# Ordering each engine's instructions with the timeline model instead of the default machine model: a delta-rule block, two MLP stages and an RWKV block on one core

## The chip, the cores and the metric

The kernel runs on 1 core of one Trainium2 chip. Its time is the device time of one execution in microseconds (us). The core has five engines that each work off a fixed list of instructions in order: TensorE (PE in the profile; its weight loads are shown as PEld), VectorE (DVE), ScalarE (ACT), GpSimd (POOL) and SyncE (SP), which here only issues transfers. Engines wait for one another through semaphores.

## What is computed

A sequence of 256 tokens of width 1024, in float32, goes through two models one after the other. All weights are float32 and are read once.

```
# first_block (DEPTH 1)
u = rms_norm(h, norm_mix);  proj = u @ w_in
pool_out = pool_mixer(proj[:, :512])                  # trailing means, a small matmul per group
q, k, v  = silu(causal_conv(proj[:, 512:2048]))       # 4 heads of 128
gdn_out  = gated_delta_net(q, k, v, z, a, b)          # chunked, a triangular solve per chunk
h = h + concat(pool_out, gdn_out) @ w_out
h = h + square(relu(rms_norm(h) @ w_up)) @ w_down     # 1024 -> 4096 -> 1024
x = rms_norm(h)
# second_block (DEPTH 2)
x = x + spatial_gating(rms_norm(x));  x = x + mlp(rms_norm(x))
x = x + rwkv7(rms_norm(x));           x = x + mlp(rms_norm(x))
out = rms_norm(x)
...
# rwkv7, per head and token t
sa = S @ (-kk_t);  S = S * w_t + sa kka_t^T + v_t k_t^T;  y_t = S @ r_t
```

## The kernel before

**Matmuls.** Each float32 operand of a large matmul is split into a high part in TensorE's float32r type and a low part that holds the rest; `split` (L205) makes them, the high part with a cast on ScalarE (L222), the low part with a subtraction on VectorE (L227; for eight RWKV weights on ScalarE and a transfer of GpSimd, L224 and L225). `mm3` (L230) then adds three matmuls: high x high (L231) and the two products of a high and a low part (L232, L233). Weights come in tiles of 1 MB from `load_ws` (L184) and `load_as` (L190), whose transfers are issued on SyncE. Raw weights, split weights, activations and PSUM tiles come from pools with a fixed number of buffers, so a load or a split waits until an older tile of its pool is released.

**Stages.** `block1` (L475) runs the projections and the delta rule on the first 150 us. The delta rule is a chain of small dependent steps on TensorE, VectorE and ScalarE: decay matrices, a triangular inverse by blocks (`eliminate`, L918; the steps Y, Z and ZT, L796 to L814), chunk state, output. The rest of the projections, the pool mixer and part of the output projection are a generator, `dense`; `fill()` pulls a few matmuls of it after each step of the chain. `mlp` (L410) runs 16 chunks of 256 hidden columns; `up(c)` is written before `down(c - 1)`. `sgu` (L968) is the spatial gating stage. `rwkv` (L1147) does the projections and decays, then a recurrence in four windows: `before`, `state`, `solve`, `update` and `output` (L1672 to L1719), each for two halves of the heads, with ScalarE copies from PSUM between the steps (L1688, L1698, L1719); its fillers are the generators `dense` and `late`. `fin` (L1721) normalises the output per head, `half_xt` (L249) transposes it, `out_mm` (L1807) projects it.

**What sets the order.** The code is written in one sequence. The framework's `TileContext` (L1919) records each instruction with its dependences and, when the context closes, decides the list of each engine: it plays the program through a model of the machine and lets each engine take, among the instructions that are ready for it in the model, the one written first. Buffers of a pool are handed out in the same pass, and semaphore waits are put in afterwards. The engines then run these lists as they are; nothing is reordered on the chip.

## Time and profile before

| | us |
|---|---|
| median of 3 runs | 1080.01 |
| lowest and highest | 1079.74 and 1084.63 |
| the profiled execution | 1082.05 |
| its span, first to last instruction | 1080.30 |
| mean granted TensorE clock, share of full speed | 0.982 |

The profile is of one execution. Its rows name an engine, a line of the kernel, the operation, and the output tile with its inputs; in a table by stretch each engine has its busy time and, in brackets, its instructions, and PEclk is the granted TensorE clock as a share of 2.4 GHz. Matmuls are pipelined, so their rows overlap: the time between two starts is what one costs.

### The profile page before, as it was taken

The page shows a single profiled execution, that of the slowest core. Times are in us where ns is not written, and L with a number is a line of the kernel's source. Part 1 is how long each engine was busy: PE and PEld are TensorE (multiplying, and loading weights), DVE is VectorE, ACT ScalarE, POOL GpSimd, SP SyncE. Part 2 cuts the span into 40 slices and gives each one's busy share as a digit, 9 for nine tenths or more (in the row PEclk, how much of TensorE's full clock was granted, in tenths as well). Part 3 has the DMA queues.
Part 4 walks back from the last instruction along what each step waited for, and adds up shares of the span by engine and source line. Part 5 has one row for each costly group of instructions (what it writes and reads, how often), then busy time and mean ns, then how long its engine had stood idle before and what let it go on. Part 6 is the DMA issues. An engine that isn't in the chain of part 4 may idle for free.

```text
span 1080.3 us, 19680 instructions
## 1 busy us (share of the span) xinstructions
PE 1049.7 (97%) x8138; PEld 939.3 (87%) x8138; DVE 726.5 (67%) x1267; ACT 560.6 (52%) x834; POOL 61.8 (6%) x102
## 2 busy tenths in 40 slices
PE   8999999999999999999999999999999989999996
PEld 6899878988898999889999998999768869999985
DVE  5889665556557886666685556998943875555565
ACT  5745454454446554455464446864535635444452
POOL 3100000000002000000000001024200000000000
PEclk9999999999999999999999999998998999999998
DMA  7343186555564745555576561445623244655531
GB/s 246 121 157 118 42 309 213 184 189 171 181 195 121 246 154 174 188 166 180 172 241 191 193 196 33 112 139 139 156 60 118 80 156 159 192 195 188 188 132 40
DMA packets 123318, 173.63 MB, mean 161 GB/s; under 512 B 6638, under 2 KB 100827, under 8 KB 122972
## 3 DMA queue, kind: packets, MB, share of 16 engines
q1 hardware_dynamic: 121930, 168.11, 48.7%
q0 software_dynamic: 1152, 4.19, 2.0%
q8 instruction: 64, 1.05, 0.4%
q14 instruction: 26, 0.21, 0.1%
q10 hardware_dynamic: 146, 0.07, 0.0%
HBM read 167.12 MB, written 1.05 MB: 156 GB/s over the span
## 4 chain that ended last, share of the span: by engine, by line
PE 83%; DVE 11%; ACT 3%; issue 1%; DMA 1%; POOL 1%; SPq 0%; ACTq 0%; POOLq 0%; DVEq 0%
PE m1a L231 3%; PE m3h L232 3%; PE m3h L233 3%; PE m1a L233 3%; PE m1a L232 3%; PE m3h L231 3%; PE m1h L232 3%; PE m2h L232 3%; PE m2h L233 3%; PE m1h L233 3%; PE m1h L231 3%; PE m2h L231 3%; PE m2a L231 3%; PE m2a L232 3%; PE m2a L233 3%; PE m3a L232 3%
## 5 line engine op out<-in xcount | busy, mean ns | idle before, releaser
L231 PE MATMUL m1h<-m1xh,m1uh 128*128 128x256 f32 x256 | 73.3, 287 | 0.0
L233 PE MATMUL m3h<-m3xh,m3ul 128*128 128x256 f32 x256 | 72.2, 282 | 0.5 <-DVE m3ul L227 0.5
L232 PE MATMUL m3h<-m3xl,m3uh 128*128 128x256 f32 x256 | 72.1, 282 | 0.3 <-DVE m3xl L391 0.3
L231 PE MATMUL m3h<-m3xh,m3uh 128*128 128x256 f32 x256 | 72.1, 282 | 0.0
L232 PE MATMUL m1h<-m1xl,m1uh 128*128 128x256 f32 x256 | 71.8, 281 | 0.2 <-DVE m1xl L391 0.2
L233 PE MATMUL m2h<-m2xh,m2ul 128*128 128x256 f32 x256 | 71.7, 280 | 0.0
L232 PE MATMUL m2h<-m2xl,m2uh 128*128 128x256 f32 x256 | 71.6, 280 | 0.0
L233 PE MATMUL m1h<-m1xh,m1ul 128*128 128x256 f32 x256 | 71.6, 280 | 0.0
L231 PE MATMUL m2h<-m2xh,m2uh 128*128 128x256 f32 x256 | 71.5, 280 | 0.0
L227 DVE TENSOR_TENSOR m3ul<-m3u,m3uh 128x1024 fp32r<-128x1024 f32 x32 | 39.2, 1225 | 47.3 <-ACT m3uh L222 47.3
L227 DVE TENSOR_TENSOR m1ul<-m1u,m1uh 128x1024 fp32r<-128x1024 f32 x32 | 39.2, 1225 | 44.9 <-ACT m1uh L222 44.8
L227 DVE TENSOR_TENSOR m2ul<-m2u,m2uh 128x1024 fp32r<-128x1024 f32 x32 | 39.1, 1225 | 35.8 <-ACT m2uh L222 35.8
L222 ACT CAST m1uh<-m1u 128x1024 fp32r<-128x1024 f32 x32 | 33.7, 1053 | 52.1 <-PE m1h L232 50.4
L222 ACT CAST m3uh<-m3u 128x1024 fp32r<-128x1024 f32 x32 | 33.5, 1048 | 51.8 <-PE m3h L232 50.0
L222 ACT CAST m2uh<-m2u 128x1024 fp32r<-128x1024 f32 x32 | 33.5, 1050 | 47.9 <-PE m2h L232 45.4
L227 DVE TENSOR_TENSOR m2dl<-m2d,m2dh 128x1024 fp32r<-128x1024 f32 x32 | 39.2, 1225 | 26.1 <-ACT m2dh L222 26.1
L227 DVE TENSOR_TENSOR m3dl<-m3d,m3dh 128x1024 fp32r<-128x1024 f32 x31 | 38.0, 1225 | 24.9 <-ACT m3dh L222 24.9
L227 DVE TENSOR_TENSOR m1dl<-m1d,m1dh 128x1024 fp32r<-128x1024 f32 x31 | 37.9, 1224 | 22.0 <-ACT m1dh L222 22.0
L222 ACT CAST m2dh<-m2d 128x1024 fp32r<-128x1024 f32 x32 | 33.6, 1050 | 33.4 <-PE m2a L233 29.9
L222 ACT CAST m1dh<-m1d 128x1024 fp32r<-128x1024 f32 x31 | 32.4, 1047 | 35.3 <-PE m1a L233 24.4
L231 PE MATMUL m2a<-m2dh,m2fh 128*128 128x512 f32 x128 | 50.1, 391 | 0.0
L222 ACT CAST m3dh<-m3d 128x1024 fp32r<-128x1024 f32 x31 | 32.7, 1054 | 33.4 <-PE m3a L233 31.6
(708 smaller groups left out, 3542.5 us busy)
## 6 DMA issues: line engine op xcount, KB each, us to landing
m1u<-in_w_up_dram SPq DMA_DIRECT2D x16, 1024.0 KB
m1d<-in_w_down_dram SPq DMA_DIRECT2D x16, 1024.0 KB, 4.9
m2u<-in_ffn_w_dram SPq DMA_DIRECT2D x16, 1024.0 KB, 6.5
m2d<-in_ffn_w_dram SPq DMA_DIRECT2D x16, 1024.0 KB, 5.5
m3u<-in_ffn_w_dram SPq DMA_DIRECT2D x16, 1024.0 KB
m3d<-in_ffn_w_dram SPq DMA_DIRECT2D x16, 1024.0 KB, 4.9
win<-in_w_in_dram SPq DMA_DIRECT2D x10, 1024.0 KB
sv<-in_sgu_w_in_dram SPq DMA_DIRECT2D x8, 1024.0 KB, 5.7
```

Source lines behind the costliest of these rows:

```text
L222: act.copy(hv, src)
L227: lo.tensor_tensor(out=lv, in0=src, in1=hv.bitcast(F32), op=ALU.subtract)
L231: pe.matmul(out, lhsT=lh, rhs=rh, start=first, stop=False)
L232: pe.matmul(out, lhsT=lh, rhs=rl, start=False, stop=False)
L233: pe.matmul(out, lhsT=ll, rhs=rh, start=False, stop=last)
```

## The change

One argument of the context is set. The code of the kernel, its tiles and its pools are the same; the model on which the framework plays the program when it decides each engine's list, and hands out the buffers, is another one, the framework's timeline model instead of its default machine model.

```diff
-    with tile.TileContext(nc) as tc:
+    with tile.TileContext(nc, schedule_with_timeline_sim=True) as tc:
         tile_two_blocks(tc, args)
```

## Rows read from the trace of the kernel before

**Rows 1.** The page: span and instructions, and each engine's busy time
```profile
span 1080.3 us, 19680 instructions
PE 1049.7 (97%) x8138; PEld 939.3 (87%) x8138; DVE 726.5 (67%) x1267; ACT 560.6 (52%) x834; POOL 61.8 (6%) x102
```

**Rows 2.** Busy time by stretch: us; PE, PEld, DVE, ACT, POOL (instructions); PEclk, DMA, GB/s
```profile
12.00:160.00 148.00, 142.30 (x1044) 130.63 (x1043) 119.80 (x307) 80.33 (x157) 10.89 (x19) 0.98 0.47 151
160.00:330.00 170.00, 170.00 (x1070) 150.99 (x1069) 96.83 (x107) 80.57 (x93) 0.95 (x1) 1.00 0.59 191
402.00:660.00 258.00, 257.75 (x1668) 233.81 (x1667) 163.67 (x193) 129.66 (x168) 2.85 (x11) 1.00 0.57 181
660.00:900.00 240.00, 227.94 (x2701) 196.17 (x2700) 180.88 (x397) 137.57 (x246) 34.88 (x50) 0.94 0.40 113
900.00:1066.00 166.00, 166.00 (x1063) 151.44 (x1063) 91.99 (x91) 78.31 (x90) 0.00 (x0) 1.00 0.52 170
1066.00:1080.30 14.30, 5.08 (x21) 3.50 (x20) 8.28 (x25) 3.77 (x10) 0.00 (x0) 0.80 0.20 74
```

**Rows 3.** The same view for the six low-clock stretches: one, and their sum
```profile
818.60:828.90 10.30, 10.23 (x133) 9.74 (x125) 4.05 (x6) 7.74 (x15) 0.00 (x0) 0.50 0.04 12
...
sum 34.20, PE 33.82 PEld 29.57 DVE 21.50 ACT 15.09 POOL 6.99; mean PE 5.64 PEld 4.93 DVE 3.58 ACT 2.52 POOL 1.16
```

**Rows 4.** First MLP: TensorE in time (start, length), groups of splits, one load
```profile
200.25 0.28 PE L231 MATMUL m1h<-m1xh,m1uh 128*128 128x256 f32 x1
200.36 0.28 PE L232 MATMUL m1h<-m1xl,m1uh 128*128 128x256 f32 x1
...
206.13 0.39 PE L232 MATMUL m1a<-m1dl,m1fh 128*128 128x512 f32 x1
206.37 0.40 PE L233 MATMUL m1a<-m1dh,m1fl 128*128 128x512 f32 x1
...
L222 ACT CAST m1uh<-m1u 128x1024 fp32r<-128x1024 f32 x32 | 33.7, 1053 | 52.1 <-PE m1h L232 50.4 <-DMA m1u<-in_w_up_dram 1.2 <-PE mo L233 0.2
L227 DVE TENSOR_TENSOR m1ul<-m1u,m1uh 128x1024 fp32r<-128x1024 f32 x32 | 39.2, 1225 | 44.9 <-ACT m1uh L222 44.8
...
m1d<-in_w_down_dram SPq DMA_DIRECT2D x16, 1024.0 KB, 4.9
```

**Rows 5.** VectorE and TensorE in time at the end of RWKV
```profile
866.14 1.22 DVE L227 TENSOR_TENSOR m3ul<-m3u,m3uh 128x1024 fp32r<-128x1024 f32 x1
...
870.78 0.68 DVE L349 TENSOR_TENSOR res<-ra,res 128x512 f32<-128x512 f32 x1
871.38 0.68 DVE L1740 TENSOR_TENSOR tBK<-tBK,V 128x512 f32<-128x512 f32 x1
...
872.21 0.63 PE L252 MATMUL yt<-ident,tBK 128*128 128x128 f32 x4 [1.99 <-DVE tBK L1740]
```

**Rows 6.** Waits of TensorE: us in total, times, longest
```profile
PE pj L233 <- DVE wil L227: 1.6, 4, 0.8
...
PE kk L1347 <- ACT sq L1343: 1.1, 1, 1.1
```

**Rows 7.** Groups of block one's triangular inverse: busy us, mean ns, idle before
```profile
L801 ACT COPY Y<-Y 128x512 f32<-128x512 f32 x6 | 3.4, 589 | 5.9 <-PE Y L799 5.9
L814 DVE TENSOR_TENSOR U<-ZT,U 128x512 f32<-128x512 f32 x6 | 4.0, 686 | 0.0
L809 DVE TENSOR_TENSOR X<-Z,X 128x512 f32<-128x512 f32 x4 | 2.7, 686 | 1.6 <-PE Z L807 1.5
```

**Rows 8.** Groups of the RWKV recurrence on ScalarE
```profile
L1719 ACT COPY tBK<-PD 64x512 f32<-64x512 f32 x8 | 4.6, 581 | 5.1 <-PE PD L1717 5.1
L1698 ACT COPY tBK<-Ud 64x512 f32<-64x512 f32 x8 | 4.6, 580 | 4.1 <-PE Ud L1696 4.0
```

**Rows 9.** ScalarE in time at block one's logarithms
```profile
33.43 1.28 ACT L699 ACT_TABLE_LOAD   x1
34.73 0.21 ACT L699 ACTIVATE gl<-ge 128x8 f32<-128x8 f32 x1
```

## The prediction, made before the change was run

> **What bounds the kernel now.** I read the page first: TensorE is busy for 1049.7 of 1080.3 us, VectorE for 67% and ScalarE for 52% [rows 1]. Then the busy time of each engine by stretch [rows 2]. Three stretches hold the three MLPs and most of the spatial gating stage (160 to 330, 402 to 660 and 900 to 1066 us): TensorE idles 0.25 us in 594. Two stretches are different. From 12 to 160 us (block one: projections and the gated delta rule) it idles 148.0 - 142.3 = 5.7 us; from 660 to 900 us (the RWKV mixer) 240.0 - 227.9 = 12.1 us. The rest of the 30.6 us of idle time is the tail after 1066 us (14.3 - 5.1 = 9.2), one chain from the last matmul to the store, and 3.4 us at the start and between the stages.
>
> The granted clock is the other loss. It is at 1.2 instead of 2.4 GHz in six stretches, 34.2 us in all, every one of them inside or just behind the two loose stretches [rows 3]; were all of it matmul time, it would cost half, 17.1 us. So the two loose stretches, 388 of 1080 us, hold 17.8 us of idle time and up to 17.1 us of slow clock: some 35 us for which the order of instructions can be held responsible.
>
> **The change, part by part.** No instruction, tile or buffer is added or taken away. The framework plays the program through a model of the machine and gives each engine, whenever that engine is free in the model, the earliest-written instruction that is ready there; that sequence is then each engine's fixed queue. With another model other instructions are ready first. What can move is seen by laying the instruction lists of the compiled kernel before beside the order in which the code writes them. TensorE's list leaves the written order 96 times among block one's 807 instructions, 87 times among RWKV's 1707, 38 times among spatial gating's 992, and 34 times in all three MLPs (3545). VectorE's does so 199 times in block one and 248 in RWKV. All five queues are re-made: SyncE's loads and GpSimd's few operations too.
>
> *The MLP stretches: 0 us.* One chunk is 48 matmuls of 256 columns, issued 0.12 us apart, and 24 of 512, 0.23 us apart [rows 4]: 5.7 + 5.6 = 11.3 us of back-to-back TensorE work, while a chunk's four casts and four subtractions take 4 x 1.05 on ScalarE and 4 x 1.22 us on VectorE. What hides their order is that they are early: ScalarE waits for TensorE to release a weight buffer (50.4 us in all for the first MLP's up weights), not the other way [rows 4]. A weight tile that is released when its matmuls end is needed again one chunk less those matmuls later, 11.3 - 2.8 = 8.5 us; cast and subtraction take 2.3, so 6 us of disorder on ScalarE or VectorE cost nothing. If that cover were gone, each microsecond beyond it would come 46 times.
>
> *SyncE's queue.* A load sits there until its buffer is free, and everything behind it waits too; who waits for that is ScalarE's cast. A load lands 4.9 us after its issue and ScalarE waited 1.2 us in all for the first MLP's up weights [rows 4]. Two neighbouring loads swapped cost nothing; I take 0 and keep the bad case as a rival.
>
> *Block one and RWKV: the terms that count.* Here the written order alternates dependent steps with filler matmuls that have nothing to do with them. What a wrong place costs is on show at 866 us. The two normalisations of the RWKV output run on VectorE, which is never idle there; a 1.22 us subtraction for the next MLP's weights and a 0.68 us residual add stand in the middle of them, and TensorE, out of other work, waits 1.99 us for the first one's last step [rows 5]. Put later, they would have saved most of the 1.99. Other long waits are for a VectorE or ScalarE step too, 1.1 and 1.6 us [rows 6]. From above: no order gets back more than the 17.8 us of idle time plus the clock's 17.1. Typically a model that is nearer to the chip would get back the waits in which something movable stood ahead; I put that at a third of the idle time, 6 us.
>
> From below there is no such bound. The dependent chains are long and each hand-over is bare when its filler has been used up elsewhere. Block one's triangular inverse has 6 copies of 0.59 us on ScalarE and 10 adds of 0.69 us on VectorE [rows 7]; these 16 are now mostly under the other half's matmuls and the filler, since TensorE idles for only 5.7 us of the stage. RWKV's recurrence has three ScalarE copies for each window and half, 24 of 0.58 us (two of the three rows of 8 are in [rows 8]), with the output projection, the gates and the other half as cover. Bare, a chain costs 16 x 0.65 = 10.4 us in block one and 24 x 0.58 = 13.9 us in RWKV. I take a third of each, 3.5 + 4.6 = 8.1 us, since each chain has three sources of cover (other half, filler, next window) and a re-made order is likely to lose about one of them in places; the ends are 0 and 24.3. The low-clock stretches lie in and behind these same chains, so I add one more of 10.3 us at half rate, 5.1 us, as the row at 818 us has it (the one at 750 us is as long) [rows 3]; ends 0 and 10.3.
>
> *ScalarE's function tables.* In block one two logarithms sit between exponentials and hyperbolic tangents, and each change of table is a load of 1.28 us [rows 9]. A tangent of the filler placed between the two logarithms adds two loads, 2.6 us on ScalarE, which is busy for 80.3 of that stage's 148 us [rows 2]; bounds 0 and 2.6, I take 0. The Trainium skill ("ScalarE: Activation LUTs", What ACT_TABLE_LOAD costs and the rule to batch calls by set) speaks against mixing them and gives about 2.66 us for every switch, the load and a drain. By that the sum would be 2 x 2.66 = 5.3 us instead of 2.6, as an estimate. The trace shows the load's 1.28 us and the next activation starting right behind it, so the lower figure agrees better.
>
> *The sum.* Bare hand-overs 8.1, slow clock 5.1, recovered waits -6, all else 0: +7.2 us. The profiled execution took 1082.05 us, 1.75 us outside its span, and lies 2.0 us above the median of the runs shown (1080.01); the sum belongs on 1082.05, which makes 1089.3, and 1087.2 beside the median. I forecast 1087.
>
> **A measure that doubts the bound.** TensorE's busy share is 95% in RWKV, but its weight loads are busy for only 196 of 240 us, 82%, against 151 of 170 us, 89%, in an MLP where it never stops [rows 2]. By that yardstick RWKV has 240 x (1 - 0.82/0.89) = 19 us to give instead of 12. The Trainium skill ("Perfetto Trace Analysis", Identifying the Most-Contended Engine) calls matmul busy time a poor measure of headroom and prefers the share of weight loading; by it the rival that comes next has more room. The trace bears that out only partly, since RWKV's many small tiles load fewer weights by nature.
>
> **The rivals.** *The nearer model wins.* The new order keeps the normalisations together, moves the reductions behind more filler and puts the clock's two 10 us stretches under denser work. It gets back half of the idle time, 8.9 us, and one of those stretches, 5.1 us: 1080.0 - 14 = 1066; with only the idle half, 1071. For it: the waits of [rows 5, 6] are mistakes of placement, which a faithful model would not make. Against it: VectorE is busy for 181 of 240 us in RWKV and without a gap around 866 us, so part of the waiting is work, not order. I put it at 1070.
>
> *Nothing that counts.* TensorE is near its limit, both models agree on what is ready, or the flag changes lists only where there is cover: 1080, within 5 us. For it: 594 us in which TensorE waits for nothing. This takes in the case that the order comes out the same.
>
> *Loads in the wrong order.* This one is slower by far: in the model a transfer is quick, so a load that must wait for a buffer is put ahead of one that TensorE needs next. Place: SyncE's queue in the MLPs; it decides once the load comes over 6 us late. Price: one microsecond beyond the cover in each of 46 chunks, 46 us, 1126. Against it: ScalarE's waits for loads are near 0 today.
>
> **How the numbers follow.** The forecast, bare hand-overs outweighing recovered waits: 0.40. Wrong loads: 0.05. Nothing that counts: 0.27. The nearer model wins: 0.28. The measurement of this kernel can tell about 0.5%, 5.4 us, from no change. So slower by over 0.5% is 0.45, within it 0.27, faster 0.28. As both signs have much of the chance, the forecast's own range is without the clock term 8.1 - 6 = 2 above the median, 1082, and with both chains bare and nothing else 1080.0 + 24.3 = 1104. The range for 8 times in 10 reaches down to 1068, below which I leave half of the nearer model's case away (about 0.1), and up to 1106, above which lie the wrong loads and a forecast with both chains bare and a slower clock (about 0.1).
>
> **What would show it.** If the forecast is right, the MLP stretches stay at full TensorE time with the same spacing, TensorE's idle time grows in block one or RWKV in waits for ScalarE copies and VectorE adds of the chains, and the low-clock time grows past 34 us. If the nearer model wins, idle time falls below 12 us together in those two stretches and the 1.99 us wait is gone. If loads are the matter, ScalarE waits for transfers in the MLPs. The prediction is wrong in its base if the MLP stretches change length, since all of them are costed at nothing.

## The result: 5% slower, and what the profile after shows

| | before | after |
|---|---|---|
| median, us | 1079.88 | 1134.64 |
| lowest and highest, us | 1078.69 to 1084.63 | 1133.28 to 1137.53 |
| ratio, 95% interval | | 1.0499, 1.0473 to 1.0524 |
| span of the profiled execution, us | 1080.3 | 1133.8 |
| mean granted TensorE clock | 0.982 | 0.963 |

The change costs 54.8 us. The forecast was 1087 us with a range up to 1106: the sign was right, the size was not.

The page of the changed kernel, the lines that answer to [rows 1]. The same instructions run, and all engines but TensorE are busy for as long as before (within 3 us).

```profile
span 1133.8 us, 19693 instructions
PE 1075.8 (95%) x8138; PEld 960.9 (85%) x8138; DVE 729.1 (64%) x1267; ACT 560.6 (49%) x834; POOL 64.2 (6%) x102
```

Busy time by stage, first the kernel before and then the changed one. The borders are the first matmul of the next stage (for the first and the third MLP that of the up projection, `m1h` and `m3h`): block one up to 148.0 (after: 169.3) us, then the first MLP, the gating stage, the second MLP and RWKV. Columns as in [rows 2].

```profile
0.00:148.00 148.00, 139.71 (x966) 122.94 (x967) 114.27 (x294) 77.56 (x147) 16.01 (x36) 0.98 0.48 153
148.00:331.80 183.80, 183.56 (x1173) 163.88 (x1172) 106.64 (x130) 89.84 (x112) 0.95 (x1) 1.00 0.61 197
331.80:477.80 146.00, 145.47 (x1040) 135.41 (x1039) 109.91 (x197) 78.55 (x110) 7.27 (x6) 1.00 0.55 175
477.80:659.40 181.60, 181.35 (x1177) 165.40 (x1176) 114.06 (x135) 94.66 (x121) 2.50 (x8) 1.00 0.57 181
659.40:890.00 230.60, 219.36 (x2634) 188.06 (x2633) 175.43 (x383) 132.09 (x236) 35.07 (x51) 0.94 0.41 116
```

```profile
0.00:169.30 169.30, 147.86 (x967) 130.01 (x968) 116.70 (x295) 77.36 (x147) 14.72 (x36) 0.93 0.43 140
169.30:355.60 186.30, 185.24 (x1177) 164.99 (x1176) 107.66 (x131) 89.73 (x112) 0.95 (x1) 1.00 0.60 190
355.60:508.90 153.30, 148.50 (x1037) 137.72 (x1035) 109.12 (x196) 78.72 (x110) 6.85 (x6) 0.98 0.54 171
508.90:695.70 186.80, 183.57 (x1177) 166.72 (x1176) 114.69 (x135) 93.98 (x121) 2.49 (x8) 0.99 0.54 171
695.70:943.00 247.30, 230.46 (x2636) 197.76 (x2635) 175.54 (x383) 133.04 (x236) 39.17 (x51) 0.91 0.39 108
```

The slow clock, the answer to [rows 3]: there were six stretches at 1.2 GHz, 34.2 us; now there are fifteen, 78.5 us (without the tail, where the clock is low in both kernels). The longest, and the sum:

```profile
862.60:876.20 13.60, 9.09 (x140) 8.64 (x142) 3.20 (x4) 6.96 (x13) 0.00 (x0) 0.50 0.40 143
...
sum 78.50, PE 71.23 PEld 62.84 DVE 50.40 ACT 24.27 POOL 5.29; mean PE 4.75 PEld 4.19 DVE 3.36 ACT 1.62 POOL 0.35
```

From these rows: idle time is length less TensorE's busy time; slow clock is what of the stretches lies in the stage, and half of what it grew by is its cost if all of it is matmul time.

| stage | longer by, us | TensorE idle | more idle | slow clock | half of its growth |
|---|---|---|---|---|---|
| block one | 21.3 | 8.3 to 21.4 | 13.1 | 6.8 to 23.9 | 8.6 |
| first MLP | 2.5 | 0.2 to 1.1 | 0.8 | 0 | 0 |
| gating | 7.3 | 0.5 to 4.8 | 4.3 | 0 to 6.8 | 3.4 |
| second MLP | 5.2 | 0.3 to 3.2 | 3.0 | 0 to 3.5 | 1.8 |
| RWKV | 16.7 | 11.2 to 16.8 | 5.6 | 27.3 to 44.3 | 8.5 |
| third MLP, tail | 0.5 | 10.1 to 10.6 | 0.6 | 0 | 0 |
| sum | 53.5 | 30.6 to 58.0 | 27.4 | 34.2 to 78.5 | 22.2 |

27.4 + 22.2 = 49.6 of the 53.5 us. This counts twice what TensorE idles within the slow stretches; TensorE's busy time in them grew by 71.2 - 33.8 = 37.4 us, half of it is 18.7, and the sum 46.1. The Trainium skill ("TensorE: Matmul & The Clock Gate", HAM oscillation) prices throttled time in the same way, by the share 1 - 1.2/2.4 of it. The trace agrees within the 4 to 7 us that are left over: in the slow stretch from 94.6 us filler matmuls of 256 columns start 0.21 us apart, right behind it 0.12.

Who TensorE waits for now (us in total, times, longest). Before, its longest single wait was 1.99 us [rows 5, 6]. The wait for `tBK` is the one of [rows 5]; it has shrunk to 0.3, as the rival "nearer model" had it, and others have come.

```profile
PE Ud L1696 <- ACT TT L1657: 3.5, 1, 3.5
PE att L828 <- ACT cv L573: 3.5, 1, 3.5
PE mo L231 <- ACT mixh L875: 3.1, 2, 1.6
PE pj L233 <- DVE wil L227: 2.9, 3, 1.5
PE ra L231 <- DVE res L349: 2.7, 1, 2.7
PE sa L231 <- ACT fh L1066: 2.6, 2, 2.4
PE ot L872 <- DVE o L866: 2.5, 1, 2.5
...
PE sp L1056 <- DVE s L1058: 1.6, 2, 0.8
...
PE PD L1717 <- ACT tBK L1719: 0.9, 2, 0.7
PE PD L1685 <- ACT xx L1688: 0.9, 2, 0.7
...
PE yt L252 <- DVE tBK L1740: 0.3, 1, 0.3
```

### The profile page after: what moved, and what is told of

The parts are those of the page before. It is cut to its first block, busy times and chain, and to the rows that moved or that the text cites. A ratio compares the mean times of both kernels' runs of the same rounds, so it can differ in the third digit from the quotient of the medians.

```text
span 1133.8 us, 19693 instructions
## 1 busy us (share of the span) xinstructions
PE 1075.8 (95%) x8138; PEld 960.9 (85%) x8138; DVE 729.1 (64%) x1267; ACT 560.6 (49%) x834; POOL 64.2 (6%) x102
## 4 chain that ended last, share of the span: by engine, by line
PE 75%; DVE 4%; ACT 2%; DMA 2%; issue 1%; ACTq 0%; SPq 0%
PE m3h L232 3%; PE m3h L233 3%; PE m3h L231 3%; PE m1h L232 3%; PE m1a L231 3%; PE m1h L233 3%; PE m1a L233 3%; PE m1h L231 3%; PE m1a L232 3%; PE m3a L231 3%; PE m3a L232 3%; PE m3a L233 3%; PE m2h L233 2%; PE m2h L232 2%; PE m2h L231 2%; PE m2a L231 2%
## 5 line engine op out<-in xcount | busy, mean ns | idle before, releaser
L231 PE MATMUL pj<-uh,wih 128*128 128x256 f32 x160 | 48.6, 304 | 4.2 <-ACT wih L222 2.4
L222 ACT CAST m1dh<-m1d 128x1024 fp32r<-128x1024 f32 x31 | 32.5, 1047 | 38.3 <-PE m1a L233 24.3
L231 PEld LDWEIGHTS m2h<-m2xh,m2uh 128*128 128x128 f32 x256 | 48.9, 191 | 1.9 <-ACT m2r L430 1.1
```

The lines of the kernel that those rows point to most:

```text
L222: act.copy(hv, src)
L231: pe.matmul(out, lhsT=lh, rhs=rh, start=first, stop=False)
```

## The first question: which engine's list

One tool serves nearly all experiments. The program is traced twice; the list of one model is read from the first tracing, and in the second, under the other model, chosen instructions are held to it by edges that set the order on an engine and wait for nothing. All that isn't held is ordered anew by the model of the second tracing. `_PIN` says what is held; `s` is the stage of an instruction by its place in the code.

```diff
+def _pin(tc, nc, other):
+    known = {i.name: i for i in nc.cur_bb.bb.instructions}
+    last = {}
+    for i in other:
+        n = _number(i.name)
+        e = str(i.engine).split(".")[-1]
+        if n is None or i.name not in known or not _PIN(e, _stage(n)):
+            continue
+        if e in last:
+            tc.add_manual_dep(
+                known[i.name], last[e],
+                mybir.DependencyInfo(mybir.DependencyClass.NoSync, mybir.DependencyReason.DATA), reason="pin",
+            )
+        last[e] = i.name
```

**TensorE's list kept.** Timeline model.

```diff
+_PIN = lambda e, s: e == 'PE'
```

> The timeline model orders everything but TensorE, whose list is held to that of the kernel before, all 8138 matmuls. Theory A (the loss of 54.8 us lies in TensorE's own list: filler taken too early, so that chain steps find no cover): the time comes back to 1080 to 1092 us and the slow-clock time to about 34 us. Theory B (it lies in the lists of VectorE and ScalarE, splits standing ahead of chain steps): 1115 to 1135 us, since those two lists are still the timeline model's. Theory C (it lies in the order of the loads): 1125 to 1135 us.

Measured: 1136.89 us, ratio 1.050 (1.046 to 1.054). Nothing came back.

**VectorE's and ScalarE's lists kept.**

```diff
+_PIN = lambda e, s: e in ('DVE', 'Activation')
```

> The opposite: the lists of VectorE and ScalarE are held to those of the kernel before, TensorE, GpSimd and SyncE are ordered by the timeline model. Theory A: nearly all of the loss stays, 1120 to 1140 us. Theory B: 1080 to 1095 us. Theory C: 1125 to 1135 us. If both lists are at fault together, this run and the one with TensorE's list held both stand between 1095 and 1120 us.

Measured: 1149.22 us, ratio 1.062 (1.058 to 1.065). Worse still.

**TensorE's new list alone**, default model for the rest.

```diff
+_PIN = lambda e, s: e == 'PE'
```

> The default model orders everything but TensorE, whose list is held to that of the changed kernel. Theory A: 1120 to 1140 us, the change's whole loss with the default model on all other engines. Theory B: 1080 to 1095 us. Theory C: 1080 to 1085 us, since the loads are those of the default model.

Measured: 1141.97 us, ratio 1.055 (1.051 to 1.060). TensorE's new list is enough for the whole loss.

**The loads' lists kept.**

```diff
+_PIN = lambda e, s: e in ('SP', 'Pool')
```

> The timeline model orders TensorE, VectorE and ScalarE; the lists of SyncE (all loads of weights) and GpSimd are held to those of the kernel before. Theories A and B: no change against the changed kernel, 1128 to 1140 us. Theory C: 1080 to 1100 us.

Measured: 1147.30 us, ratio 1.059 (1.054 to 1.064).

No theory of one guilty list survives: A falls with the first run, B with the second and third, C with the third and fourth; where a theory had the sign right, the time was still 2 to 14 us above what it gave. TensorE's new list does the harm by itself, and with TensorE's old list the lists that the timeline model makes for VectorE and ScalarE do as much. Hence a fourth theory, J: the three lists are one whole, made for one another.

**Three lists kept.** The timeline model still orders SyncE and GpSimd and hands out the buffers.

```diff
+_PIN = lambda e, s: e in ('PE', 'DVE', 'Activation')
```

> The timeline model still decides SyncE, GpSimd and the buffers; the lists of TensorE, VectorE and ScalarE are all three held to those of the kernel before. With TensorE's list alone held the time was 1136.9 us, with VectorE's and ScalarE's alone 1149.2, with the loads' alone 1147.3. Theory J (the loss is that the three lists no longer fit one another, so that it is whole as soon as one of them is re-made): 1078 to 1088 us, everything comes back. Theory S (it is not in those lists but in what the model hands out besides, buffers and the waits that come with them): 1125 to 1150 us.

Measured: 1083.05 us, ratio 1.0041 (1.0021 to 1.0062). All but 0.4% is back, as theory J has it: the loss lies in the three lists together. Loads, GpSimd and buffers under the new model cost some 4 us together, and holding lists costs nothing beyond that. That the lists don't fit one another is a reading, and can't be all of it: the changed kernel's three lists were made together too and lose as much, and lists that weren't held were ordered beside the held one. VectorE's or ScalarE's list alone was new in no run.

## The second question: which stage, and do the prices add

**Block one kept**, all five lists; then **RWKV kept**.

```diff
+_PIN = lambda e, s: s == 'b1'
```

> All five lists are held to those of the kernel before for the instructions of block one and for no others. Stages apart (each stage has its own loss): the first matmul of the first MLP comes at 148 to 150 us instead of 169.3, and the time is 1135 - 21 = 1114 us, 1108 to 1120. Stages coupled (a later stage gives the gain back or takes a new loss): the first MLP at 148 to 150 us all the same, the time above 1120 us.

Measured: 1122.42 us, ratio 1.040 (1.0375 to 1.0423).

```diff
+_PIN = lambda e, s: s == 'rwkv'
```

> The same for the instructions of the RWKV stage alone. Stages apart: from the second MLP's end to the third MLP's first matmul 230.6 us as before instead of 247.3, and the time is 1135 - 17 = 1118 us, 1111 to 1124. Stages coupled: above 1124 us.

Measured: 1123.10 us, ratio 1.040 (1.0375 to 1.0424). Both give back 12 us where 21 and 17 were expected: the first stands on the coupled side of its mark, the second just on the other. Then the other way round, one stage new and all else held to the lists before: **block one new**, **gating new**, **RWKV new** and **the three MLPs new**.

```diff
+_PIN = lambda e, s: s != 'b1'
```

> All five lists are those of the kernel before except for the instructions of block one, which the timeline model orders. TensorE's list in block one is then the changed kernel's. Stage prices add: the first MLP starts 21 us late as in the changed kernel, nothing is lost behind it, 1098 to 1106 us. With TensorE's new list and the default model on the other engines block one cost 27.8 us (1109.9 us in all): if VectorE's and ScalarE's new lists fit TensorE's new one better than the default's do, this is 4 to 9 us less; if they add harm of their own, it is more than 1110 us.

```diff
+_PIN = lambda e, s: s != 'sgu'
```

> The same with the gating stage alone new. Stage prices add: 7 us, from the stage's first transposes to those of the second MLP, 1085 to 1092 us. If the loss seen there belonged to the border with the second MLP, whose lists are old here: within 4 us of the kernel before.

```diff
+_PIN = lambda e, s: s != 'rwkv'
```

> The same with RWKV alone new. Stage prices add: 12 to 17 us, 1092 to 1099 us (16.6 us from the second MLP's end to the third's first matmul in the changed kernel, 5 of which were the border with the third MLP). Coupled: if RWKV's new lists don't fit the third MLP's old ones, 20 us or more, above 1101 us.

```diff
+_PIN = lambda e, s: s in ('b1', 'sgu', 'rwkv')
```

> Block one, gating and RWKV keep all five lists of the kernel before; the three MLPs have those that the timeline model makes. If the MLPs are covered, as the prediction has it (0 us): 1080 to 1085 us. If what the changed kernel lost in the two stretches of the first and second MLP (2.5 and 5.3 us by the first matmuls of the stages) is the MLPs' own: 1086 to 1092 us. If the stages are coupled at their borders (splits of the next MLP among the last steps of a chain): above that.

Measured, with the length of each stage of the profiled execution as its difference to the kernel before (from the first matmul of a stage to that of the next):

| run | median, us | ratio | block one | MLP 1 | gating | MLP 2 | RWKV | MLP 3, tail |
|---|---|---|---|---|---|---|---|---|
| changed kernel | 1134.64 | 1.050 | +21.3 | +2.6 | +7.2 | +5.3 | +16.6 | +0.6 |
| block one kept | 1122.42 | 1.040 | +2.6 | +3.4 | +7.3 | +4.3 | +20.4 | +0.9 |
| RWKV kept | 1123.10 | 1.040 | +20.3 | +3.7 | +7.8 | +3.1 | +6.6 | +0.6 |
| block one new | 1102.54 | 1.0208 (1.0167 to 1.0249) | +21.1 | 0.0 | 0.0 | 0.0 | +4.7 | -0.1 |
| gating new | 1094.68 | 1.0130 (1.0110 to 1.0149) | +3.0 | +1.0 | +6.9 | 0.0 | +2.4 | 0.0 |
| RWKV new | 1103.09 | 1.0207 (1.0187 to 1.0228) | -2.2 | 0.0 | +0.1 | 0.0 | +26.6 | 0.0 |
| MLPs new | 1094.89 | 1.0125 (1.0090 to 1.0160) | -2.6 | +3.4 | 0.0 | +3.1 | +5.1 | +2.1 |
| TensorE kept | 1136.89 | 1.050 | +11.3 | +0.2 | +5.1 | +1.6 | +36.0 | +0.2 |

Where a stage's lists are the old ones, and its neighbours' too, its length is the old one to 0.1 us, apart from block one and RWKV, which move by up to 3 and 5 us with the same lists (RWKV by 8.7 us in the profiled execution of "three lists kept", the slowest of its ten; its loads were new): these two have the slow clock. With TensorE's list alone kept, block one's price halves and RWKV's doubles; that run is no mixture of good and bad stages. Each new stage carries its own price, in the stage where it was expected: block one 21.1, gating 6.9, RWKV 26.6.

Two times were missed: gating new took 1094.68 us instead of 1085 to 1092, since block one, the first MLP and RWKV were 3.0, 1.0 and 2.4 us longer with lists that were held, and why stays open; RWKV new lies above 1101 us, the mark of the coupled case.

The MLPs are not free: 3.4 and 3.1 us in the first and second, and 5.1 us in RWKV, at whose end the third's splits already stand among the last steps of the chain. The 5.1 are no scatter of the clock: TensorE idles there 17.1 us instead of 11.2, 4.1 of them in one wait of `ra` for a residual add that was 0.8, while the slow clock is 27.3 us as before. That end lies in a stage whose lists were kept, so it is the coupling at the border that was named as the third case.

The prices alone sum to 21.1 + 6.9 + 26.6 + 13.7 = 68 us, more than the 53.5 of all together. They don't add, mostly because RWKV costs 26.6 us alone and 16.6 in the changed kernel. The profiled execution of RWKV new is the slowest of four, 3.5 us above their median, but the medians, each beside the kernel before of the same day, don't add either: 22.5 + 14.7 + 23.1 + 12.2 = 72.5 us beside 54.8. The trace shows a part: with RWKV alone new, TensorE waits 6.0 us once for a ScalarE copy at the end of the recurrence, which it doesn't in the changed kernel (RWKV new, TensorE's waits):

```profile
PE yt L252 <- ACT tBK L1698: 6.0, 1, 6.0
```

Why that end comes out better when the neighbours are new as well stays open.

## The third question: what in the lists

**Filler taken early.** TensorE's list of block one, read in time order, with the filler (576 matmuls, of `pj` and `mo`) counted ahead of each step of the chain:

| step of the chain | filler ahead of it, before | after |
|---|---|---|
| `KK`, first half | 178 | 242 |
| `fold`, second half (the inverse's input) | 266 | 328 |
| first `Y` (the inverse is known) | 478 | 480 |
| `kc` (state) | 485 | 528 |
| `ot`, second half (output) | 528 | 543 |

In RWKV, of 636 filler matmuls (projections and the small products for decays and gates), 172 went before the first `kk` and now 240, 474 before the last `AB` and now 531. In time (start, length) around the inverse, before:

```profile
64.17 0.96 PE L770 MATMUL fold<-cc,ab 128*128 128x16 f32 x8
66.81 0.17 DVE L925 TENSOR_TENSOR elp<-elb,A 128x8 f32<-128x8 f32 x1
90.76 0.27 DVE L928 TENSOR_TENSOR X<-X,elp 128x120 f32<-128x120 f32 x1
```

and after:

```profile
70.05 0.68 DVE L766 TENSOR_TENSOR ab<-AT,cc 128x512 f32<-128x512 f32 x1
74.05 0.96 PE L770 MATMUL fold<-cc,ab 128*128 128x16 f32 x8
75.37 0.18 DVE L925 TENSOR_TENSOR elp<-elb,A 128x8 f32<-128x8 f32 x1
101.24 0.28 DVE L928 TENSOR_TENSOR X<-X,elp 128x120 f32<-128x120 f32 x1
```

The operand of `fold` is ready at 70.73 and the matmul starts at 74.05: 3.3 us later (0.6 before), behind filler that stood ahead of it in the list and kept TensorE busy without a gap. VectorE's elimination takes 24.2 us before and 26.1 after, but 212 filler matmuls lay over it before and 152 now (480 - 328), some 18 us at 0.12 each. The rest is bare: TensorE waits 1.0, 0.8 and 3.5 us between 92 and 102 us, with two stretches of slow clock. The same at the output: between `kc` and the second `ot` there were 43 matmuls of 0.23 us, and 15 are left; `ot` now waits 2.5 us for VectorE and `mo` 3.1 us for ScalarE.

**TensorE's new list in one stage**, with the default model on all other engines: block one, then RWKV.

```diff
+_PIN = lambda e, s: e == 'PE' and s == 'b1'
```

> The kernel before with its default model, but TensorE's list in block one is that of the changed kernel: 62 more filler matmuls ahead of the last fold (328 instead of 266 of 576) and 43 more ahead of the first matmul of the state (528 instead of 485). Cover spent early: the 62 (0.12 us each) put the inverse off by 7 us, and the 152 left, 18 us, don't cover its 24; the output steps lose their 43 (0.23 us each); block one gets 20 to 28 us longer, everything behind it is as before, 1100 to 1110 us. If instead TensorE's list does harm only together with the other lists of the timeline model: under 1090 us.

```diff
+_PIN = lambda e, s: e == 'PE' and s == 'rwkv'
```

> The kernel before with its default model, TensorE's list in RWKV held to that of the changed kernel. If TensorE's list alone carries the price, as in block one: 12 to 20 us, 1092 to 1101 us. If it is splits and adds placed ahead of the chain's steps on VectorE and ScalarE: less than 6 us, under 1087 us.

Measured: 1109.92 us (1.0244, 1.0215 to 1.0273) with block one 27.8 us longer and nothing behind it by more than 0.8; 1099.57 us (1.0173, 1.0150 to 1.0196) with RWKV 20.4 us longer. Both sizes are as expected, and in both stages TensorE's list alone is enough for the price. But the waits, first of block one and then of RWKV, show that the way was only partly the one expected:

```profile
PE pj L233 <- DVE wil L227: 7.4, 5, 4.0
PE pj L231 <- ACT wih L222: 5.8, 3, 3.0
```

```profile
PE yt L252 <- DVE tBK L1740: 7.4, 1, 7.4
```

In block one VectorE starts its elimination at 79.4 us, 12.6 late, as the early filler has it. It then takes only 18.0 us and ends at 97.3, and TensorE's next step, `xt`, still comes at 111.6 instead of 91.7. In the time between, TensorE works for half:

```profile
97.30:111.60 14.30, 7.22 (x38) 6.58 (x38) 8.28 (x22) 6.10 (x10) 0.00 (x0) 0.75 0.28 99
```

The filler ahead of `xt` in its list waits there 5.0 us for weights that VectorE and ScalarE, in their default order, split later (13.2 in all of block one), and `att` 2.1 us for ScalarE. So early filler costs twice: what stands behind it in the list is late, and it must itself wait if the other lists weren't made for it. With all lists of the timeline model the second part is smaller: block one is 21.1 us longer instead of 27.8. That is the fit that theory J speaks of, here worth 6.7 us; the 21.1 us remain with lists that were made together.

**A split ahead of a step of the chain.** The same thing on ScalarE and VectorE. In the changed kernel, in time, with the wait in brackets; first the end of the inverse, then RWKV's recurrence:

```profile
99.02 1.99 ACT L222 CAST woh<-wo 128x1024 fp32r<-128x1024 f32 x2 [1.45 <-DMA wo<-in_w_out_dram]
100.10 1.23 DVE L227 TENSOR_TENSOR wol<-wo,woh 128x1024 fp32r<-128x1024 f32 x1 [0.92 <-ACT woh L222]
102.29 2.08 PE L828 MATMUL att<-qT,kT 128*128 128x128 f32 x8 [3.45 <-ACT cv L573]
...
866.45 1.99 ACT L222 CAST rwoh<-rwo 128x1024 fp32r<-128x1024 f32 x2 [3.56 <-DMA rwo<-in_rwkv_w_o_dram]
868.47 2.35 ACT L1657 COPY TT<-Uc 32x512 f32<-32x512 f32 x4
869.68 3.67 PE L1696 MATMUL Ud<-xx,TT 64*64 64x64 f32 x32 [3.47 <-ACT TT L1657]
```

ScalarE stands before a cast whose load hasn't landed. In RWKV the last input of the copies behind it, which TensorE needs, is there at 865.8 us; behind 3.56 us of waiting and two casts of 1.0 us they start 2.7 us later, and TensorE waits 3.47 us. The longest slow stretch (862.6 to 876.2) lies here. I moved twelve such splits (the expectation counts ten) behind the steps that they stood ahead of, and left all lists otherwise as the timeline model made them (numbers are instructions in the code's order).

```diff
+_MOVES = [
+    ("Activation", [1567, 1549], 1380), ("DVE", [1568, 1550], 925), ("Activation", [1644, 1614], 1476),
+    ("DVE", [1645, 1615], 1505), ("DVE", [4403, 4407], 4285), ("Activation", [9143, 9182], 8851),
+]
```

> All five lists are those of the changed kernel, but for ten splits of weights that stood ahead of a step of a chain and now stand right behind it: in block one four casts of the output projection on ScalarE and their four subtractions on VectorE (two subtractions of 1.23 and 1.22 us stood between the last steps of the triangular inverse at 100 to 102 us, two casts waited 6.27 us for a load at 137.6 us ahead of the copies of the state), in the gating stage two subtractions of 1.2 us at 425.7 and 427.2 us, in RWKV two casts at 866.5 us that waited 3.56 us for their load ahead of four copies. Theory H (a split ahead of a step of a chain makes TensorE wait for it, and the step that was ready goes as soon as the split is gone): block one 2 to 4 us shorter, gating 1.5 to 2.5, RWKV 2.5 to 3.5, and a few us less of slow clock; together 1117 to 1129 us against 1135. Theory A' (only TensorE's own list matters by now; the splits are hidden): 1132 to 1138 us.

Measured: 1132.87 us, ratio 1.0453 (1.0426 to 1.0481) beside 1.0499 of the changed kernel: about 5 us, but the intervals overlap, so the gain is not clear of noise. 1132.87 us lies above the range of theory H and in that of theory A'. Block one is 4.6 us shorter in the profiled execution, the fastest of five, gating 0.1 and RWKV 1.0; and in block one that is clock and not cover, since TensorE idles there 24.5 us instead of 21.4, with 10.2 us of slow clock instead of 23.9. Theory H is right that the wait behind each moved split goes, and wrong on what that brings. TensorE's waits in this kernel, for gating, RWKV and block one:

```profile
PE sa L233 <- DVE fl L1067: 2.2, 1, 2.2
...
PE Ud L1696 <- ACT xx L1688: 2.0, 1, 2.0
...
PE Z L807 <- ACT Y L801: 3.1, 1, 3.1
```

Each is new: the splits, one step later, now stand ahead of the next step. Instead of 1.6 us for `s` TensorE waits 2.2 for `fl` (the 2.4 for `fh` lie later, behind a split that I hadn't moved, and are still there), instead of 3.5 for `TT` 2.0 for `xx`, instead of 3.5 for `cv` ahead of `att` 3.1 for `Y`; and the wait for `mixh` grew from 3.1 to 5.0. A split has to go somewhere, and in these places, without cover, the next one cost as well.

## The fourth question: one unlucky list, or the model

The fill counts of the code could be fitted to the default model's order. So the same other counts under both models:

```diff
-    'n': [1, 0, 5, 3, 7, 5, 4, 4, 0, 1, 9, 2, 2, 1, 2, 2, 0, 0, 8, 13],
+    'n': [3, 3, 3, 3, 3, 3, 3, 3, 3, 3, 3, 3, 3, 3, 3, 3, 3, 3, 3, 3],
...
-    'fl': [4, 4, 4, 2, 4, 2, 16, 8],
+    'fl': [8, 8, 8, 8, 8, 8, 8, 8],
```

> The kernel before with its default model and other counts of filler: three after each step of block one's chain instead of 0 to 13, and one for every 8 heads in the RWKV recurrence instead of one for 2 to 16. The lists are re-made, TensorE's with some 680 lines of difference, VectorE's with 470. Theory L (the filler counts are fitted to the default model's order, so any re-made order loses tens of us, whatever the model): 1105 to 1140 us. Theory G (the timeline model's play itself makes worse lists for this program): within 1075 to 1095 us.

> The changed kernel with the other counts of filler that cost the kernel before 10 us (1.0104 times its time). Theory G (the timeline model's play makes worse lists of this program, whatever the counts): 1120 to 1165 us, 35 us or more above the same program under the default model. Theory L (the changed kernel's lists are one unlucky draw, which other counts of filler mend): 1085 to 1115 us.

Measured: default model 1089.83 us (1.0104, 1.0077 to 1.0132), timeline model 1149.51 us (1.059, 1.054 to 1.064). Theory G: under either set of counts the timeline model's order is some 50 to 60 us slower. This clears one set of lists of bad luck; it doesn't say what in that model makes it take filler earlier, which no run here looked into.

## Why the prediction was right in sign and wrong in size

The sign came out right, in part by luck: the term that carried it, bare hand-overs, hardly came; other waits and the clock did.

- **What bounds the kernel** (two loose stretches, idle time and slow clock): right as a picture. 38.0 of the 53.5 us came from block one and RWKV, and 35.8 of these are idle time and half of the slow clock.
- **"The MLP stretches: 0 us".** Inside, it held: chunks keep their spacing, 0.12 us for 256 columns, and ScalarE still waits 50.0 us for TensorE in all, not the other way, the line that answers to [rows 4]:

```profile
L222 ACT CAST m1uh<-m1u 128x1024 fp32r<-128x1024 f32 x32 | 33.5, 1052 | 50.8 <-PE m1h L232 50.0 <-DVE mixl L876 0.8
```

  It failed at the borders and in gating. The stretch from 402 to 660 us held gating's second half, and its 0.25 us of idle time was taken as cover; but its chain (`sp`, `s`, `fh`, `sa`) was covered by order alone, like the other two. TensorE's old list left the written order 38 times in its 992 matmuls; I counted these and priced them at nothing. It was 6.9 us. The MLPs, new alone, cost 3.4, 3.1 and 5.1 us. In the first two that lies in their first chunks: in the first MLP a cast that waits 3.00 us for its tile stands ahead of the first `m1r`, and TensorE waits 1.1 us for that. The prediction's own sign of a wrong base, that the MLP stretches change length, came true.
- **"SyncE's queue: 0".** Held: with the three other lists old, the new order of the loads, GpSimd and the buffers cost 0.4% together. What I left out is that a load's time matters through ScalarE: casts of weights that hadn't landed were put ahead of copies. The waits for the loads of `wo` and `rwo` were 0 before; now `rwo` has the 3.56 us above, and `wo`:

```profile
ACT woh L222 <- DMA wo<-in_w_out_dram: 7.7, 2, 6.3
```

- **"Bare hand-overs: 3.5 + 4.6 = 8.1, ends 0 and 24.3".** This step failed, in its place more than in its size. TensorE's idle time grew by 13.1 us in block one and 5.6 in RWKV, 18.7, which lies between the ends, but not at the hand-overs that were priced. For the 16 of the inverse TensorE still waits under 0.1 us; for the three copies of the recurrence 1.8 us (the two `PD` rows above) instead of 1.2. What ran is the general form ("its filler has been used up elsewhere") at other places. In block one TensorE waits 9.0 us for `cv`, `mixh` and `o`, for which it did not wait before, and its filler waits 7.1 instead of 2.9 us for split weights (`wil`, `wih`, `wol`, `woh`); in RWKV it waits 3.5 us for `TT`, and `ra` 6.1 instead of 1.5 us for the residual add, `yl` and `yh`. Two things were missing. The largest piece of block one's cover, 212 matmuls over VectorE's 24 us elimination, wasn't among my 16 hand-overs of [rows 7]; and I priced lost cover only, not the delay of a chain step behind filler in the same queue (3.3 us for one `fold`). The share of a third (one source of cover out of three) had no row behind it. The lines that answer to [rows 7, 8] are waits of ScalarE and VectorE for TensorE. In the inverse they grew, from 5.9 to 8.6 us ahead of the `Y` copies and from 0 to 4.8 ahead of the `U` adds, as steps behind filler or at the slow clock would have it; in the recurrence one row grew, from 4.1 to 6.2, and one fell, from 5.1 to 3.3.

```profile
L801 ACT COPY Y<-Y 128x512 f32<-128x512 f32 x6 | 3.5, 585 | 8.6 <-PE Y L799 8.6
L1698 ACT COPY tBK<-Ud 64x512 f32<-64x512 f32 x8 | 4.6, 579 | 6.2 <-PE Ud L1696 6.2
L1719 ACT COPY tBK<-PD 64x512 f32<-64x512 f32 x8 | 4.6, 578 | 3.3 <-PE PD L1717 3.3
L814 DVE TENSOR_TENSOR U<-ZT,U 128x512 f32<-128x512 f32 x6 | 4.1, 688 | 4.8 <-PE ZT L812 4.8
```

- **"Slow clock: one more stretch, 5.1 us".** The term that was furthest off: nine more stretches, 44.3 us more in all, 22.2 at half rate (18.7 by TensorE's busy time in them), and three of the fifteen lie in gating and the second MLP, where there was none. I had tied the clock to two places, and the new order made waits in others.
- **"Recovered waits: -6 us".** Wrong. The 1.99 us of [rows 5] did go to 0.3, 1.7 us; right behind it TensorE now waits 2.7 us for a residual add and 1.9 for `yl`.
- **Tables: 0.** Held: five loads of 1283 ns in each kernel.
- **The rivals.** "The nearer model wins" had 0.28 and rested on the waits of [rows 5, 6] being mistakes that another model would not make; the new list made others. "Nothing that counts" had 0.27 for the 594 us without waits; a stretch without waits can be one whose order is right. "Wrong loads" came nearest in size, 46 us, with the wrong place.
- **The base.** The sum added up single hand-overs, waits and shares of cover. The runs show that an order isn't such a sum: TensorE's list alone, or all lists but TensorE's, cost about as much as all together, and the prices of the stages don't add.

## What to carry to other kernels

Where engines work off fixed lists, an order is one object: here TensorE's list from another model cost as much alone as all of them together, so hold or change them together and stage by stage. A stretch without waits says that its order is good, not that it is safe; price a re-made order by all the filler that lies over chains now, and by the filler that may come to stand ahead of a chain step in the same queue, and add the clock that the new gaps slow. To find which list costs what, hold a chosen engine or stage to the other order by order-only edges; the one mend of single instructions that was tried mostly moved the wait to the next step.

## What the runs showed of the hardware that I had not expected

In these runs the slow clock doesn't follow the total of idle time. The kernel with other fill counts under the default model has 41.1 us of idle time, 10.5 more than the kernel before (page: span 1085.8, TensorE busy 1044.7), yet its slow stretches, apart from the tail, sum to 20.5 us instead of 34.2:

```profile
sum 20.50, PE 19.95 PEld 15.99 DVE 12.62 ACT 4.70 POOL 3.75; mean PE 3.99 PEld 3.20 DVE 2.52 ACT 0.94 POOL 0.75
```

The mean granted clock of its four executions was 0.982 to 0.990, that of thirteen of the kernel before on the same day 0.980 to 0.988: with more idle time it is no lower.

And the same five lists for RWKV took 230.7 us in the kernel before, 233.0 with gating new and 235.4 with block one new, while every MLP with old lists and old neighbours repeated to 0.1 us. In the last of the three TensorE idles as long as before (11.3 us, before 11.2), and 41.0 us are slow instead of 27.3, so the 4.7 us are the clock's. In these traces a stage that TensorE never leaves idle repeats, and one with short gaps has several us of scatter, so single profiles of such stages shouldn't be read more finely than that.
